# RWKV layer: elementwise work of the channel-major stage from GpSimd to VectorE, and score products that alternate between the halves of TensorE's rows

## The chip, the cores and the metric

The kernel runs on one core of one Trainium2 chip. The metric is the device time of one execution in microseconds (us). Five engines work side by side, each through its own list of instructions in order: TensorE (PE in the profile; PEld is its weight load), VectorE (DVE), ScalarE (ACT), GpSimd (POOL) and SyncE (SP), which here issues the weight transfers. An instruction waits on semaphores until its operands are there and its output buffer is free.

## The reference, cut to what matters

A trunk of two layers over 512 tokens of 1024 channels, in float32. Each layer is a half-step SwiGLU feed-forward, a token mixer, cross-attention into 256 memory tokens, and another half-step feed-forward. The mixer of the first layer is RWKV-7, that of the second a chunked gMLP. The change lies in RWKV-7 alone, which has 16 heads of 64 channels:

```python
dx = token_shift(h) - h
xr, xw, xk = h + dx*mu[0], h + dx*mu[1], h + dx*mu[2]
xv, xa, xg = h + dx*mu[3], h + dx*mu[4], h + dx*mu[5]
x3 = jnp.stack([xr, xk, xv], axis=0)
rkv = jnp.einsum('nbsc,cnd->nbsd', x3, w_rkv.reshape(C, 3, C))
...
k = k * (1.0 + (a - 1.0) * k_a)
def step(state, inp):
    r_t, w_t, k_t, v_t, kk_t, b_t = inp
    sa = jnp.einsum('bhij,bhj->bhi', state, -kk_t)
    state = (state * w_t[:, :, None, :] + sa[..., None] * b_t[:, :, None, :]
             + v_t[..., :, None] * k_t[:, :, None, :])
    y = jnp.einsum('bhij,bhj->bhi', state, r_t)
    return state, y
```

The recurrence over 512 steps is the scan. The result is normalised per head, gated and multiplied by `w_o`.

## The kernel before, in words

A program is nine stages: feed-forward, RWKV, attention, feed-forward, feed-forward, gMLP, attention, feed-forward, final norm. Every large product is made of three: an operand is split into a rounded part `hi`, cast by ScalarE (L93), and the rest `lo = raw - hi`, by VectorE (L98) or, in pieces of 512 columns, by GpSimd (L96); `mm3` then adds hi*hi, hi*lo and lo*hi (L114 to L116). `wload` brings a piece of weight by DMA and splits it. A scheduler puts each engine's instructions into one order from the priorities of the code and its own estimates; it can move them across each other where data allow. A wait at the head of an engine's list holds all that stands behind it.

RWKV works in two parts. In the channel-major stage, channels lie on the partitions and tokens along the rows of a tile. First the token-shift difference `dx` (L908, 16 operations of 128x256) and the three mixes made from it (L911) feed the small decay, rate and gate products (L913 to L916). Then the projections of k, r and v follow, 48 steps of one piece of 512 columns of `w_rkv`: `prepare` loads and splits the weight of a step, and for the first of the two column blocks it makes the mix `xm` (L837), casts it (L862) and subtracts (L863, tile `xs`). The projections' outputs go to `AR` and `BK`, eight tiles of each, 128 channels apiece. Work on finished k blocks is done by generators that are advanced between projection steps: `post_k(nb)` multiplies by rates and decays (L1000 to L1002; the norm of each head goes through TensorE as `pn`, L977; then L1037 to L1039), `post_r(nb)` does r's part (L1052, L1056). For each half `q` of the heads, a triangular inverse of 32x32 blocks is worked out on VectorE by substitution, 30 pairs of L1188 and L1195 whose widths go from 60 and 31 up to 256 and down again, and the blocks are put together on TensorE (L1227). Its result is `TT`.

The scan goes in chunks: 8 per half of the heads, 16 in all, so the loop has 16 steps, `n = 0..15`. A step multiplies the state and values `SV` by the score tile `M` (L1448, first solve product), copies the result to `e1`, multiplies by `TT` (L1464), copies that to `AV` (L1466 VectorE, L1467 ScalarE), updates the state (L1482), and makes the output (L1517, L1518). Meanwhile it prepares the next step: `score(n+1)` multiplies `BK` and `AR` for the two halves of the partitions, `par` 0 and 1, in four products each (L1286), masks them into `M` (L1288, VectorE) and copies two parts (L1289, L1290, ScalarE); `decayed` scales `BK` on GpSimd (L1295); `turned` transposes it (L1301). Between the pieces, `next(fill)` puts in independent products of the memory's keys and values (L114 to L116 with `mT`), and `pump()` advances the gate and normalisation (L1318 to L1321). The scan's first scores are made in `prologue`, while the second inverse still runs. PSUM tiles called `sc` come from a pool of two buffers. `rows[par]` are partitions 0 to 63 and 64 to 127; a product whose operands lie in them uses that half of TensorE's rows.

Of the kernel before, what the change touches and what calls it, by code (L numbers as in the profile page):

```python
# [9 lines left out]
F32 = mybir.dt.float32  # L10
F32R = mybir.dt.float32r
AF = mybir.ActivationFunctionType
ALU = mybir.AluOpType
# [5 lines left out]
T = 512  # L19
# [7 lines left out]
NCH = T // CH  # L27
# [12 lines left out]
class Trunk:  # L40
# [763 lines left out]
    def rwkv_in(self, st, prologue):  # L804

        nc, ins = self.nc, self.ins
        col = lambda i, ct: self.cols[:, i, ct : ct + 1]
        hT = self.hT
        AR, BK = self.AR, self.BK
        self.psp = self.pool(st, "psr", 5, space=PSUM)  # L810
        acc = self.pool(st, "acc", 1, space=PSUM)
        sc = self.sc
# [38 lines left out]
        def prepare(i):  # L851
            if i >= len(steps):
                return
            p, nb, k = steps[i]
            m, wi = projs[p]
            late = p == 2 or (p == 1 and k == 1)
            src = ins["rwkv_w_rkv"][wi, nb, k // 2][:, (k % 2) * 512 : (k % 2) * 512 + 512]
            ws[i] = self.wload(src, 512, nc.gpsimd if late else nc.vector)
            if nb == 0:
                xm = xmix(m, k)  # L860
                xh = xsp.tile([P, 2, T], F32R, tag="xs", name="xs")
                nc.scalar.copy(xh[:, 0], xm)  # L862
                nc.gpsimd.tensor_tensor(xh[:, 1], xm, xh[:, 0].bitcast(F32), ALU.subtract)  # L863
                xs[p, k] = xh[:, 0], xh[:, 1]
# [33 lines left out]
        for half in range(2):  # L898
            s = slice(256 * half, 256 * half + 256)
            for ct in range(KC):  # L900
# [4 lines left out]
                with self.tc.high_priority(offset=60 if early else 0):  # L905
                    dx = room(n)
                    eng = nc.vector if early else nc.gpsimd
                    eng.tensor_tensor(dx, hT[:, ct, s], h, ALU.subtract)  # L908
                    xw, xa, xg = [room(n + j) for j in (1, 2, 3)]
                    for m, z in ((1, xw), (4, xa), (5, xg)):  # L910
                        nc.vector.scalar_tensor_tensor(z, dx, col(MU + m, ct), h, ALU.mult, ALU.add)  # L911
# [77 lines left out]
        def post_k(nb):  # L989
            pn = acc.tile([P, 512], F32, tag="acc", name="pn")  # L990

            def part(i):
# [7 lines left out]
                nc.vector.tensor_tensor(fe, fe, em, ALU.mult)  # L1000
                nc.gpsimd.tensor_tensor(a, a, c3(em), ALU.mult)
                nc.vector.tensor_tensor(c3(fe), raw, c3(fe), ALU.mult)  # L1002
# [23 lines left out]
            for i in range(4):  # L1026
# [10 lines left out]
                nc.vector.scalar_tensor_tensor(c3(kn), raw, nkk[:, ct : ct + 1], c3(ps), ALU.mult, ALU.mult)  # L1037
                nc.gpsimd.tensor_tensor(raw, c3(kn), c3(ep[:, 0:T]), ALU.mult)
                nc.vector.tensor_tensor(a, a, c3(kn), ALU.mult)  # L1039
# [196 lines left out]
    def rwkv_scan(self, st):  # L1236
# [42 lines left out]

        def score(n, M, par):  # L1280

            q, c = divmod(n, NCH)
            ps = sc().rearrange("p (k j) -> p k j", k=4)
            for i in range(4):
                ct = 4 * q + i
                mm(ps[:, i], BK[ct][rows[par], c, :], AR[ct][rows[par], c, :], start=True, stop=True)  # L1286
            mA = self.con[:, I_MA : I_MA + P].unsqueeze(1).to_broadcast([P, 4, P])
            nc.vector.tensor_tensor(M[:, par], ps, mA, ALU.mult)  # L1288
            nc.scalar.copy(M[rows[par], par, :, 0:64], self.ARq[q][rows[par], :, c, 0:64])  # L1289
            nc.scalar.copy(rz[n % 2][rows[par], par], self.ARq[q][rows[par], :, c, 64:128])  # L1290

# [68 lines left out]
        def prologue():  # L1360
# [5 lines left out]
            yield  # L1366
            score(0, M, 0)
            yield
            score(0, M, 1)
            decayed(0)  # L1370
# [53 lines left out]
        for n in range(2 * NCH):  # L1424
# [30 lines left out]
            if not end:  # L1455
                score(n + 1, nm, 0)
            next(fill, None)
            pump()
            for s in range(2):
# [7 lines left out]
                nc.scalar.copy(AV[rows[1], 1, cs, :], p2[rows[1]])  # L1467
            if not end:
                score(n + 1, nm, 1)
                if c + 2 != NCH:  # L1470
                    decayed(n + 1)
            next(fill, None)
# [260 lines left out]
```

## Time and profile before

| what | value |
|---|---|
| median of 3 runs | 2445.85 us (2445.23 to 2446.88) |
| the profiled execution's own time | 2445.8 us |
| its span in the trace | 2444.0 us |
| mean granted TensorE clock, share of full speed | 0.992 |
| busy: PE / DVE / ACT / POOL | 2382.0 / 1690.0 / 1087.3 / 236.6 us |
| chain that ended last: PE / DVE / ACT | 88% / 6% / 2% |
| the RWKV channel-major stage | 365 to 645 us |
| its scan | 645 to 818 us |

The profiled execution agrees with the median; 1.8 us of its time lie outside the span. TensorE is busy for 97% of the span, but that is a mean over stages: the waits are nearly all in the channel-major stage. Busy times of engines overlap, so they don't add up to the span.

### The profile page before, as it was taken

The numbers are of one execution on the slowest core, as the hardware profiler recorded it, in microseconds if no ns is written. First come the engines' busy times: TensorE is split into PE (matmuls) and PEld (weight loads), VectorE is DVE, ScalarE is ACT, GpSimd is POOL, SyncE is SP. The second block draws the span as 40 slices with busy tenths as digits, with TensorE's granted clock in tenths as the row PEclk, the third lists the DMA queues.
The fourth block names the chain that finished last, engine by engine and source line by source line (L and its number), as shares of the span: only waits on it lengthen the run. The fifth ranks groups of instructions, "written<-read, shape, count | busy, mean of one in ns | idle before, by whom it ended". The sixth has DMA issues, their size and how long they took to land.

```text
span 2444.0 us, 40275 instructions
## 1 busy us (share of the span) xinstructions
PE 2382.0 (97%) x16336; PEld 2085.6 (85%) x16336; DVE 1690.0 (69%) x2607; ACT 1087.3 (44%) x1821; POOL 236.6 (10%) x230
## 2 busy tenths in 40 slices
PE   7999999888899999999999999999999999999998
PEld 7898985656787888989898999998888888989897
DVE  7776858788767655969595877674253464969594
ACT  5343434875455344535254534343342343535252
POOL 2000004433345200000000000000000000000000
PEclk9999999999999999999999999999999999999999
DMA  4433232111434432233232324242322232233232
GB/s 148 142 100 121 87 102 72 61 44 57 123 87 120 154 101 74 83 102 120 78 125 94 118 70 130 78 151 86 104 87 88 85 121 82 70 104 112 93 95 86
DMA packets 104938, 241.66 MB, mean 99 GB/s; under 512 B 27184, under 2 KB 31280, under 8 KB 104368
## 3 DMA queue, kind: packets, MB, share of 16 engines
q1 hardware_dynamic: 98864, 225.67, 29.3%
q10 hardware_dynamic: 5888, 13.42, 1.7%
q8 instruction: 128, 2.10, 0.4%
q14 instruction: 58, 0.48, 0.1%
HBM read 227.38 MB, written 7.34 MB: 96 GB/s over the span
## 4 chain that ended last, share of the span: by engine, by line
PE 88%; DVE 6%; ACT 2%; issue 1%; DMA 1%; POOL 1%; DVEq 0%; POOLq 0%; SPq 0%; ACTq 0%
PE ps L114 27%; PE ps L116 27%; PE ps L115 27%; PE sc L1286 1%; DVE tmp L1188 1%; PE ps L217 1%; DVE X L1195 1%; PE y L1517 1%; DVE AR L911 1%; PE y L1518 1%; DVE wlo L98 1%; PE ps L756 1%; POOL wlo L96 0%; PE sm L1448 0%; DMA m_scr<-mo 0%
## 5 line engine op out<-in xcount | busy, mean ns | idle before, releaser
L98 DVE TENSOR_TENSOR wlo<-wraw,whi 128x1024 fp32r<-128x1024 f32 (+1 forms) x246 | 277.4, 1131 | 296.9 <-ACT whi L93 278.3
L114 PE MATMUL ps<-nT_hi,whi 128*128 128x256 f32 (+1 forms) x1504 | 449.6, 301 | 3.5 <-ACT nT_hi L93 1.5
L116 PE MATMUL ps<-nT_hi,wlo 128*128 128x256 f32 (+1 forms) x1504 | 448.4, 299 | 1.2 <-POOL wlo L96 1.2
L115 PE MATMUL ps<-nT_lo,whi 128*128 128x256 f32 (+1 forms) x1504 | 449.0, 299 | 0.4 <-DVE nT_lo L98 0.3
L93 ACT CAST whi<-wraw 128x1024 fp32r<-128x1024 f32 (+1 forms) x268 | 245.9, 921 | 370.6 <-PE ps L116 237.5
L114 PEld LDWEIGHTS ps<-nT_hi,whi 128*128 128x128 f32 x1504 | 283.1, 189 | 15.1 <-ACT nT_hi L93 3.2
L115 PEld LDWEIGHTS ps<-nT_lo,whi 128*128 128x128 f32 x1504 | 284.4, 189 | 10.8 <-DVE nT_lo L98 1.5
L116 PEld LDWEIGHTS ps<-nT_hi,wlo 128*128 128x128 f32 x1504 | 284.0, 189 | 11.3 <-POOL wlo L96 1.5
L116 PE MATMUL ps<-whi,hT_lo 128*128 128x512 f32 x704 | 278.2, 395 | 0.0
L114 PE MATMUL ps<-whi,hT_hi 128*128 128x512 f32 x704 | 278.0, 395 | 0.0
L115 PE MATMUL ps<-wlo,hT_hi 128*128 128x512 f32 x704 | 277.9, 395 | 0.0
L116 PE MATMUL ps<-s_hi,wlo 128*128 128x256 f32 x960 | 271.2, 283 | 1.2 <-DVE wlo L98 1.1
L114 PE MATMUL ps<-s_hi,whi 128*128 128x256 f32 x960 | 271.0, 282 | 1.3 <-ACT whi L93 0.7
L115 PE MATMUL ps<-s_lo,whi 128*128 128x256 f32 x960 | 270.3, 282 | 0.0
L93 ACT CAST whi<-g_raw 128x1024 fp32r<-128x1024 f32 x160 | 168.1, 1050 | 201.7 <-PE ps L116 135.6
L98 DVE TENSOR_TENSOR wlo<-g_raw,whi 128x1024 fp32r<-128x1024 f32 x160 | 195.4, 1221 | 33.2 <-ACT whi L93 32.3
L116 PEld LDWEIGHTS ps<-s_hi,wlo 128*128 128x128 f32 x960 | 181.6, 189 | 2.0 <-DVE wlo L98 2.0
L114 PEld LDWEIGHTS ps<-s_hi,whi 128*128 128x128 f32 x960 | 181.7, 189 | 1.7 <-ACT whi L93 0.9
L115 PEld LDWEIGHTS ps<-s_lo,whi 128*128 128x128 f32 x960 | 181.4, 189 | 0.0
L197 POOL TENSOR_TENSOR rs<-ms,mhalf 128x1 f32<-128x1 f32 x42 | 26.1, 622 | 1391.2 <-DVE ms L191 1391.2
L116 PEld LDWEIGHTS ps<-whi,hT_lo 128*128 128x128 f32 x704 | 132.5, 188 | 30.9
L115 PEld LDWEIGHTS ps<-wlo,hT_hi 128*128 128x128 f32 x704 | 132.6, 188 | 30.7
(360 smaller groups left out, 4870.7 us busy)
## 6 DMA issues: line engine op xcount, KB each, us to landing
wraw<-in_ffn_w_out_dram SPq DMA_DIRECT2D x88, 512.0 KB, 4.1
g_raw<-in_ffn_w_in_dram SPq DMA_DIRECT2D x80, 512.0 KB, 3.7
t_raw<-in_ffn_w_in_dram SPq DMA_DIRECT2D x80, 256.0 KB, 3.0
e_raw<-in_ffn_w_in_dram SPq DMA_DIRECT2D x80, 256.0 KB, 3.4
wraw<-in_rwkv_w_rkv_dram SPq DMA_DIRECT2D x48, 256.0 KB, 2.8
wraw<-in_ffn_w_in_dram SPq DMA_DIRECT2D x16, 512.0 KB, 3.6
wraw<-in_xattn_wq_dram SPq DMA_DIRECT2D x16, 512.0 KB, 3.6
wraw<-in_xattn_wo_dram SPq DMA_DIRECT2D x16, 512.0 KB, 3.5
```

The lines of the kernel that those rows point to most:

```text
L93: r = [self.nc.scalar.copy(hi, src)]
L98: r.append(self.nc.vector.tensor_tensor(lo, src, hi.bitcast(F32), ALU.subtract))
L114: mm(ps, l[0], r[0], start=start, stop=False, **kw)
L115: mm(ps, l[0], r[1], start=False, stop=False, **kw)
L116: mm(ps, l[1], r[0], start=False, stop=stop, **kw)
L197: self.nc.gpsimd.tensor_tensor(rs, ms, self.mhalf[:, 0:1], ALU.pow)
L217: nc.tensor.transpose(ps[:, j * P : (j + 1) * P], xn[:, k * P : (k + 1) * P], self.ident)
L756: nc.tensor.matmul(pv[:, t * P : (t + 1) * P], v[:, t, g * P : (g + 1) * P], ws[:, g, :], start=True, stop=True,)
L911: nc.vector.scalar_tensor_tensor(z, dx, col(MU + m, ct), h, ALU.mult, ALU.add)
L1188: nc.vector.tensor_tensor(tv, M2[:, s + 1 : 32, s : s + 1].to_broadcast([P, n, s + 1]), X[:, s : s + 1, 0 : s + 1].to_broadcast([P, n, s + ...
L1195: nc.vector.tensor_tensor(xs, xs, tv, ALU.add)
L1286: mm(ps[:, i], BK[ct][rows[par], c, :], AR[ct][rows[par], c, :], start=True, stop=True)
```

## The change

Five places in the channel-major stage that used GpSimd for an elementwise operation use VectorE: the `lo` split of the 18 late weights, the 24 `xs` subtractions, 15 of the 16 `dx`, and the products L1001 and L1038 (8 each). In the scan, `score` is called once per step, after the first solve product: it takes two `sc` tiles and issues its eight products with `par` alternating, then does both masks and the copies. `decayed` stays behind the second solve product. Lines behind 863 move by 1 to 3; those behind the loop in `score` too.

```diff
--- before.py
+++ after.py
@@ -853,14 +853,13 @@
                 return
             p, nb, k = steps[i]
             m, wi = projs[p]
-            late = p == 2 or (p == 1 and k == 1)
             src = ins["rwkv_w_rkv"][wi, nb, k // 2][:, (k % 2) * 512 : (k % 2) * 512 + 512]
-            ws[i] = self.wload(src, 512, nc.gpsimd if late else nc.vector)
+            ws[i] = self.wload(src, 512)
             if nb == 0:
                 xm = xmix(m, k)
                 xh = xsp.tile([P, 2, T], F32R, tag="xs", name="xs")
                 nc.scalar.copy(xh[:, 0], xm)
-                nc.gpsimd.tensor_tensor(xh[:, 1], xm, xh[:, 0].bitcast(F32), ALU.subtract)
+                nc.vector.tensor_tensor(xh[:, 1], xm, xh[:, 0].bitcast(F32), ALU.subtract)
                 xs[p, k] = xh[:, 0], xh[:, 1]
 
 
@@ -904,8 +903,7 @@
                 early = half == 0 and ct < 1
                 with self.tc.high_priority(offset=60 if early else 0):
                     dx = room(n)
-                    eng = nc.vector if early else nc.gpsimd
-                    eng.tensor_tensor(dx, hT[:, ct, s], h, ALU.subtract)
+                    nc.vector.tensor_tensor(dx, hT[:, ct, s], h, ALU.subtract)
                     xw, xa, xg = [room(n + j) for j in (1, 2, 3)]
                     for m, z in ((1, xw), (4, xa), (5, xg)):
                         nc.vector.scalar_tensor_tensor(z, dx, col(MU + m, ct), h, ALU.mult, ALU.add)
@@ -998,7 +996,7 @@
                 act(em, L[:, ct, :], AF.Exp, scale=DECAY)
                 act(c3(fe), a, AF.Identity, scale=col(KA, ct), bias=oka[:, ct : ct + 1])
                 nc.vector.tensor_tensor(fe, fe, em, ALU.mult)
-                nc.gpsimd.tensor_tensor(a, a, c3(em), ALU.mult)
+                nc.vector.tensor_tensor(a, a, c3(em), ALU.mult)
                 nc.vector.tensor_tensor(c3(fe), raw, c3(fe), ALU.mult)
                 halved(ct, 0, c3(fe))
                 return sq
@@ -1035,7 +1033,7 @@
                 kn = tmp("fe")[:, :T]
                 raw, a = AR[ct][:, :, 0:64], AR[ct][:, :, 64:128]
                 nc.vector.scalar_tensor_tensor(c3(kn), raw, nkk[:, ct : ct + 1], c3(ps), ALU.mult, ALU.mult)
-                nc.gpsimd.tensor_tensor(raw, c3(kn), c3(ep[:, 0:T]), ALU.mult)
+                nc.vector.tensor_tensor(raw, c3(kn), c3(ep[:, 0:T]), ALU.mult)
                 nc.vector.tensor_tensor(a, a, c3(kn), ALU.mult)
                 halved(ct, 1, a)
                 yield
@@ -1277,17 +1275,19 @@
         def new_m(n):
             return cps[n % 2].tile([P, 2, 4, P], F32, tag="M", name="M")
 
-        def score(n, M, par):
+        def score(n, M):
 
             q, c = divmod(n, NCH)
-            ps = sc().rearrange("p (k j) -> p k j", k=4)
+            pss = [sc().rearrange("p (k j) -> p k j", k=4) for _ in range(2)]
             for i in range(4):
                 ct = 4 * q + i
-                mm(ps[:, i], BK[ct][rows[par], c, :], AR[ct][rows[par], c, :], start=True, stop=True)
+                for par, ps in enumerate(pss):
+                    mm(ps[:, i], BK[ct][rows[par], c, :], AR[ct][rows[par], c, :], start=True, stop=True)
             mA = self.con[:, I_MA : I_MA + P].unsqueeze(1).to_broadcast([P, 4, P])
-            nc.vector.tensor_tensor(M[:, par], ps, mA, ALU.mult)
-            nc.scalar.copy(M[rows[par], par, :, 0:64], self.ARq[q][rows[par], :, c, 0:64])
-            nc.scalar.copy(rz[n % 2][rows[par], par], self.ARq[q][rows[par], :, c, 64:128])
+            for par, ps in enumerate(pss):
+                nc.vector.tensor_tensor(M[:, par], ps, mA, ALU.mult)
+                nc.scalar.copy(M[rows[par], par, :, 0:64], self.ARq[q][rows[par], :, c, 0:64])
+                nc.scalar.copy(rz[n % 2][rows[par], par], self.ARq[q][rows[par], :, c, 64:128])
 
         def decayed(n):
             q, c = divmod(n, NCH)
@@ -1364,9 +1364,8 @@
             cur = load_v(0)
             M = new_m(0)
             yield
-            score(0, M, 0)
-            yield
-            score(0, M, 1)
+            score(0, M)
+            yield
             decayed(0)
             yield
             self.mem_load()
@@ -1453,7 +1452,7 @@
                     nc.vector.tensor_copy(e1, p1)
                 es.append(e1)
             if not end:
-                score(n + 1, nm, 0)
+                score(n + 1, nm)
             next(fill, None)
             pump()
             for s in range(2):
@@ -1465,10 +1464,8 @@
                 cs = slice(2 * s, 2 * s + 2)
                 nc.vector.tensor_copy(AV[rows[0], 0, cs, :], p2[rows[0]])
                 nc.scalar.copy(AV[rows[1], 1, cs, :], p2[rows[1]])
-            if not end:
-                score(n + 1, nm, 1)
-                if c + 2 != NCH:
-                    decayed(n + 1)
+            if not end and c + 2 != NCH:
+                decayed(n + 1)
             next(fill, None)
             pump()
             if not last:
```

Where the instructions stand. The first place is on TensorE, in one scan step of the second half of the heads: `sm` are the PSUM tiles of the small products, `sc` those of the scores, and `ps` with `whi` and `mT` are fill. A tile's size in such a row is the space it is given, not what one product writes. Before:

```order
L1448 MATMUL sm_8104<-SV_7956,M_7962 64x64 x4
L1286 MATMUL sc_8111<-AR1_3886,BK1_3894 128x128 x4
L114 MATMUL ps_7732<-whi_7987,mT_6158 128x512
...
L1464 MATMUL sm_8133<-e1_8102,TT1_6916 64x64 x4
L1464 MATMUL sm_8140<-e1_8109,TT1_6916 64x64 x4
L1286 MATMUL sc_8147<-AR1_3886,BK1_3894 128x128 x4
L114 MATMUL ps_7733<-whi_7987,mT_6158 128x512
L115 MATMUL ps_7733<-wlo_7988,mT_6158 128x512
L116 MATMUL ps_7733<-whi_7987,mT_6158 128x512
L1482 MATMUL sm_8162<-AV_7957,BT_8079 64x64 x4
```

Now:

```order
L1447 MATMUL sm_8104<-SV_7956,M_7962 64x64 x4
L1285 MATMUL sc_8111<-AR1_3886,BK1_3894 128x128
L1285 MATMUL sc_8112<-AR1_3886,BK1_3894 128x128
L1285 MATMUL sc_8111<-AR1_3886,BK1_3894 128x128
L1285 MATMUL sc_8112<-AR1_3886,BK1_3894 128x128
...
L1285 MATMUL sc_8112<-AR1_3886,BK1_3894 128x128
L114 MATMUL ps_7740<-whi_7995,mT_6158 128x512
...
L1463 MATMUL sm_8141<-e1_8102,TT1_6916 64x64 x4
L1463 MATMUL sm_8148<-e1_8109,TT1_6916 64x64 x4
L114 MATMUL ps_7741<-whi_7995,mT_6158 128x512
...
L114 MATMUL ps_7740<-whi_8048,mT_6158 128x512
L1479 MATMUL sm_8162<-AV_7957,BT_8079 64x64 x4
```

The second group of four scores has gone from behind L1464 (now L1463) to the first, where they alternate between two `sc` tiles; between L1463 and L1479 (before L1482) there is fill alone.

The second place is on VectorE where `post_k(0)` begins, with the splits of projection weights around it. Before:

```order
L98 TENSOR_TENSOR wlo<-wraw,whi 128x512
L947 SCALAR_TENSOR_TENSOR L<-fe,sq 128x512
L1000 TENSOR_TENSOR fe<-fe,em 128x512
L98 TENSOR_TENSOR wlo<-wraw,whi 128x512
L1002 TENSOR_TENSOR fe<-AR_3885,fe 128x512
L98 TENSOR_TENSOR wlo<-wraw,whi 128x512
L1000 TENSOR_TENSOR fe<-fe,em 128x512
L1002 TENSOR_TENSOR fe<-AR_3885,fe 128x512
L837 SCALAR_TENSOR_TENSOR xm_4779<-hT,omu,xm_4777 128x512
```

Now:

```order
L98 TENSOR_TENSOR wlo<-wraw,whi 128x512
L945 SCALAR_TENSOR_TENSOR L<-fe,sq 128x512
L998 TENSOR_TENSOR fe<-fe,em 128x512
L999 TENSOR_TENSOR AR_3885<-AR_3885,em 128x8x64
L1000 TENSOR_TENSOR fe<-AR_3885,fe 128x512
L98 TENSOR_TENSOR wlo<-wraw,whi 128x512 x2
L998 TENSOR_TENSOR fe<-fe,em 128x512
L999 TENSOR_TENSOR AR_3885<-AR_3885,em 128x8x64
L1000 TENSOR_TENSOR fe<-AR_3885,fe 128x512
L862 TENSOR_TENSOR xs<-xm_4655,xs 128x512
L862 TENSOR_TENSOR xs<-xm_4704,xs 128x512
L837 SCALAR_TENSOR_TENSOR xm_4779<-hT,omu,xm_4777 128x512
```

L999 (before L1001 on GpSimd) stands between L998 and L1000, which do not need it, and two `xs` subtractions (L862, before L863 on GpSimd) and more `wlo` splits are in line.

The third place is on VectorE in the second inverse (`tmp`, `X`), where the first scores of the scan are masked into `M`. Before:

```order
L1195 TENSOR_TENSOR X<-X,tmp 128x9x23
L1188 TENSOR_TENSOR tmp<-M_5896,X 128x192
L1195 TENSOR_TENSOR X<-X,tmp 128x8x24
L1188 TENSOR_TENSOR tmp<-M_5896,X 128x175
L1195 TENSOR_TENSOR X<-X,tmp 128x7x25
L1188 TENSOR_TENSOR tmp<-M_5896,X 128x156
L98 TENSOR_TENSOR mT<-mraw,mT 128x512
L1288 TENSOR_TENSOR M<-sc,con 128x512 x2
L98 TENSOR_TENSOR mT<-mraw,mT 128x512
L1195 TENSOR_TENSOR X<-X,tmp 128x6x26
```

Now:

```order
L1193 TENSOR_TENSOR X<-X,tmp 128x17x15
L98 TENSOR_TENSOR wlo<-wraw,whi 128x512
L1186 TENSOR_TENSOR tmp<-M_5896,X 128x256
L1193 TENSOR_TENSOR X<-X,tmp 128x16x16
L1186 TENSOR_TENSOR tmp<-M_5896,X 128x255
L1193 TENSOR_TENSOR X<-X,tmp 128x15x17
L1186 TENSOR_TENSOR tmp<-M_5896,X 128x252
L98 TENSOR_TENSOR mT<-mraw,mT 128x512
L98 TENSOR_TENSOR wlo<-wraw,whi 128x512
L1288 TENSOR_TENSOR M<-sc,con 128x512 x2
L98 TENSOR_TENSOR mT<-mraw,mT 128x512
L1193 TENSOR_TENSOR X<-X,tmp 128x14x18
```

The masks L1288 stand behind the step of 252 elements, where they stood behind that of 156; in between there are `wlo` splits that GpSimd did before.

## Rows read from the trace of the kernel before

**Rows 1.** Windows by stage: us, busy time of each engine (instructions), PEclk, DMA share, GB/s.
```profile
365.00:645.00 280.00, 245.08 (x1709) 168.74 (x1708) 225.97 (x348) 168.97 (x293) 113.81 (x103) 0.94 0.21 64
645.00:818.00 173.00, 171.75 (x2145) 143.96 (x2143) 125.05 (x247) 89.58 (x213) 82.00 (x72) 1.00 0.41 104
```

In these rows the engines are in the order PE, PEld, DVE, ACT, POOL.

**Rows 2.** Windows inside the channel-major stage, same columns.
```profile
365.00:470.00 105.00, 102.10 (x479) 67.04 (x478) 80.66 (x116) 65.58 (x112) 45.33 (x44) 1.00 0.21 67
470.00:500.00 30.00, 23.30 (x304) 14.63 (x302) 19.14 (x23) 22.72 (x40) 15.23 (x15) 0.77 0.12 37
500.00:565.00 65.00, 53.65 (x193) 36.29 (x194) 63.90 (x111) 42.42 (x72) 22.17 (x19) 0.95 0.18 57
597.00:645.00 48.00, 41.35 (x188) 32.40 (x179) 40.66 (x75) 15.89 (x30) 16.31 (x15) 0.93 0.33 98
```

**Rows 3.** Groups of POOL, 365 to 645: busy us, mean ns | idle before, releaser.
```profile
L863 POOL TENSOR_TENSOR xs<-xm,xs 128x512 fp32r<-128x512 f32 x24 | 37.0, 1546 | 43.5 <-ACT xs L862 43.4
L96 POOL TENSOR_TENSOR wlo<-wraw,whi 128x512 fp32r<-128x512 f32 x18 | 24.5, 1364 | 55.2 <-ACT whi L93 52.4 <-issue 2.8
L1001 POOL TENSOR_TENSOR AR<-AR,em 128x512 f32<-128x512 f32 x8 | 14.8, 1850 | 28.0 <-ACT fe L999 22.5 <-DVE wlo L98 5.5
L1038 POOL TENSOR_TENSOR AR<-fe,em 128x512 f32<-128x512 f32 x8 | 12.0, 1502 | 3.5 <-DVE fe L1037 3.1
```

**Rows 4.** Groups of DVE, 365 to 645, same columns.
```profile
L1188 DVE TENSOR_TENSOR tmp<-M,X 128x60 f32<-128x60 f32 (+15 forms) x60 | 29.3, 489 | 1.3
L98 DVE TENSOR_TENSOR wlo<-wraw,whi 128x512 fp32r<-128x512 f32 x32 | 26.8, 841 | 8.3 <-ACT whi L93 4.3 <-POOL rz L1383 4.0
L1195 DVE TENSOR_TENSOR X<-X,tmp 128x60 f32<-128x60 f32 (+15 forms) x60 | 25.6, 426 | 1.2
L837 DVE SCALAR_TENSOR_TENSOR xm<-hT,omu,xm 128x512 f32<-128x512 f32 x24 | 23.6, 1000 | 2.5 <-POOL xs L863 2.4
L911 DVE SCALAR_TENSOR_TENSOR AR<-AR,cols,hT 128x256 f32<-128x256 f32 x45 | 22.2, 561 | 0.1
```

**Rows 5.** Single lines, 365 to 645: duration ns min/median/max, first and last start.
```profile
L1000 DVE TENSOR_TENSOR fe<-fe,em x8: 676/932/1820, 450.0 to 515.8; 128x512 f32<-128x512 f32 x8
L837 DVE SCALAR_TENSOR_TENSOR xm<-hT,omu,xm x24: 735/748/1781, 406.7 to 592.7; 128x512 f32<-128x512 f32 x24
L911 DVE SCALAR_TENSOR_TENSOR AR<-AR,cols,hT x45: 469/477/1397, 381.0 to 411.6; 128x256 f32<-128x256 f32 x45
```

**Rows 6.** Timeline of DVE in the second inverse: start, duration.
```profile
617.56 0.42 DVE L1195 TENSOR_TENSOR X<-X,tmp 128x256 f32<-128x256 f32 x1
```

**Rows 7.** The chain that ended last, 450 to 542: start, us, what.
```profile
450.00 1.80 POOL AR L1001
...
462.09 1.73 POOL xs L863
...
498.68 1.83 DVE fe L1000
...
541.12 1.49 DVE X L1195
```

**Rows 8.** Waits of PE, 365 to 645: us, times, longest.
```profile
PE sc L1301 <- DVE M L1288: 6.7, 1, 6.7
```

**Rows 9.** Timeline of PE in one scan step: start, us from the first to the last end.
```profile
769.58 0.68 PE L1464 MATMUL sm<-e,TT 64*64 64x64 f32 x16
770.19 1.16 PE L1286 MATMUL sc<-AR,BK 64*128 64x128 f32 x8
771.27 0.50 PE L114 MATMUL ps<-whi,mT 128*128 128x512 f32 x1
...
772.17 0.69 PE L1482 MATMUL sm<-AV,BT 128*64 128x64 f32 x16
```

**Rows 10.** Timelines of DVE and ACT in the same step.
```profile
771.38 0.69 DVE L1288 TENSOR_TENSOR M<-sc,con 128x512 f32<-128x512 f32 x1
...
770.60 0.46 ACT L1467 COPY AV<-sm 64x128 f32<-64x128 f32 x2 [1.55 <-DVE AV L1466]
```

## Prediction

> **What bounds the kernel now.** I read the busy time by stage first. The feed-forward, attention and gMLP parts ahead of 365 us and behind 818 us hold none of the edited lines, so I leave them as they are. In the 173 us of the scan TensorE is busy 171.75: it has no slack, and only less work on TensorE shortens it. In the 280 us of the channel-major stage ahead TensorE is busy 245.08, so 35 us are waits; VectorE (DVE) is busy 225.97, GpSimd (POOL) 113.81 [rows 1].
>
> Next I cut that stage where its character changes. From 365 to 470 TensorE is busy 102.10 of 105: the other engines hide behind the projections. From 470 to 500 it is idle 6.7 of 30, and its mean granted clock is 0.77. From 500 to 565 VectorE is busy 63.90 of 65, so VectorE sets the pace. From 597 to 645 TensorE is idle 6.65 of 48 [rows 2]. These three stretches are where the moved operations can matter.
>
> The groups of GpSimd's work say what is moved, and what it waited for: the `xs` and `wlo` subtractions wait mostly for ScalarE's casts, 43.4 and 52.4 us in total, L1001 22.5 for ScalarE too [rows 3]. GpSimd has time for that.
>
> **What the moved operations cost VectorE.** By the diff 24 + 18 + 8 + 8 = 58 operations of 128x512 and 15 of 128x256 change engine. VectorE does a 128x512 product or difference undisturbed in 676 ns (the shortest L1000 [rows 5]) to 0.69 us (L1288 [rows 10]), and 128x256 in 0.42 [rows 6]. So 58 x 0.69 + 15 x 0.42 = 40.0 + 6.3 = 46.3 us are added.
>
> **What it gets back.** The same L1000 that takes 676 ns at best takes 1820 at worst, and L837 and L911 have as wide a spread in one shape [rows 5]; the long ones coincide with a GpSimd operation with two inputs. Mean less minimum, times the count: L98 32 x (841 - 676) = 5.3; L837 24 x (1000 - 735) = 6.4; L911 45 x (561 - 469) = 4.1 [rows 4, 5]; L1000 by its median 8 x (932 - 676) = 2.0 [rows 5]. The 120 inverse operations (L1188, L1195) have sizes from 31 to 256 elements, 181 in the mean; at 0.42 us for 256 I estimate 0.35 undisturbed, so 60 x (0.489 - 0.35) + 60 x (0.426 - 0.35) = 12.9 come back, and at least 4.5 if 0.42 held for all [rows 4, 6]. These five come to 30.7 (22.3 at least). So VectorE is loaded by at most 46.3 - 22.3 = 24 us more over the stage, and I take some 10, since groups that I don't list (L1039, L1056) are stretched too. Against that 88 us of slow GpSimd work (37.0 + 24.5 + 14.8 + 12.0 [rows 3]) no longer stands between producer and reader: one takes 1.36 to 1.85 us there and 0.69 on VectorE.
>
> The Trainium skill, SBUF — State Buffer, "Who interferes with whom", says that a VectorE instruction with two SBUF inputs and a GpSimd one that reads SBUF exclude each other for the whole instruction. The trace agrees on which operations are stretched. By the rule alone up to 88 us of VectorE time could come back, twice what is added; the rows give about a third of that, because GpSimd often runs while VectorE waits, and I go by the rows.
>
> **Where that falls.** Four terms:
> - 365 to 470: the 15 differences add 6.3 us to a chain of L911, which gets back 4.1. TensorE has 2.9 us of idle time in all [rows 2], most of it there. I take 1 us lost (0 to 2).
> - 470 to 500: what arrives late here was made between 450 and 470, where the chain runs through GpSimd: L1001 at 450.00 for 1.80 us and `xs` at 462.09 for 1.73, the first and last of four such links [rows 7]. Each is 1.0 shorter on VectorE, so 4 us, of 6.7 that TensorE idles. I take 4 (0 to 7). The second excerpt of the order, on VectorE, shows the other side: L999 and L862 stand in line there, where nothing stood.
> - 500 to 565: VectorE is the pace. The chain has six stretched operations in it, L1000 with 1.83 the first and an inverse step with 1.49 the last, each about 1.0 over its undisturbed time [rows 7]: 6 come back on the chain, and the four L1038 here and their kin are 0.7 shorter each. Against it 14 moved operations of 0.69 (9.7). Between -4 and +7 I take 2.
> - 597 to 645: TensorE's longest wait of the stage is here, 6.7 us, L1301 for the masked scores of L1288 [rows 8], which stand in VectorE's queue behind the second inverse. The third excerpt of the order shows them after the step of 252 elements instead of after that of 156: 16 inverse operations of about 0.40 fewer ahead, 6.4 us. In the whole order six `wlo` splits (three in the excerpt) are new ahead of them inside this inverse, 4.1 us, and about half of the inverses' 12.9 is returned. 6.4 - 4.1 + 6 is more than the wait itself holds; since ahead of the inverse three more splits and five `xs` were put in, partly in idle time, I take 4 (-3 to 6.7).
>
> Sum for the stage: -1 + 4 + 2 + 4 = 9 us gained, bounds -9 and +21.
>
> **The score products.** In each of the 15 loop steps that have a successor, TensorE so far does one group of four products after the first solve product and another after the second, 1.08 us each (770.19 to 771.27, [rows 9]). In a group the products use one half of the rows and follow one another. After the change, eight products stand together, the halves taking turns, into two PSUM tiles. The trace has no such pair of 64 rows by 128 columns, only the nearest thing: the 64x64 products of L1464, which alternate between halves. Their 16 records take 0.61 us (769.58 to 770.19), 0.038 each; L1286's eight take 1.08, 0.135 each, 3.5 times as long for twice the columns. So an alternating pair should cost about as much as one product now, and eight products 1.08 instead of 2.16: 15 x 1.08 = 16.2 us. If halves do not overlap, only a change-over to another kind of product goes, for which I allow 0.2 per step (an estimate: L1464's whole 0.61 leaves no room for much more), 3 us. I take the first, because L1464 shows halves at work at the same time.
>
> What this takes away is cover. TensorE's L1482 needs `AV`, copied from the second solve product. Before, the other score group and a fill (1.08 + 0.90) stood between; now the fill alone, 771.27 to 772.17 [rows 9]. VectorE's two mask products (2 x 0.69), then two ScalarE copies, come ahead of the last `AV` copy (2 x 0.23, [rows 10]). From the scores' end: 1.38 + two copies at 0.4 (an estimate from the 0.46 of [rows 10]) + 0.46 = 2.65; TensorE reaches L1482 after fill, solve and fill, 0.90 + 0.61 + 0.90 = 2.4, later in steps with gate products. So 0.25 per step, 4 us over 15. The scan gains 16 - 4 = 12 (0 to 16).
>
> The Trainium skill, TensorEngine Tiling (Array Packing), "PSUM Bottleneck", says that tiling speeds TensorE but not the evacuation, which may become the bound. By that rule the scan would be paced by the four copies, worked out from rows as the second rival below.
>
> **The sum.** 9 + 12 = 21: 2445.8 (the profiled execution's own time, 1.8 of it outside the span and untouched; the median is 2445.85, so it is a typical one) - 21 = 2424.8 us.
>
> **The rivals.**
> - *The halves do not overlap* (0.14): each score record takes its 0.13 us whichever half. The stage gains 9, the scan 3: 2434. For it: no 64x128 pair is in the trace. Against it: L1464.
> - *The copies pace the scan* (0.15): `AV` is late by 1 us in each step rather than 0.25, because the mask products and the copies in front of it run one after the other over two engines. Then 15 of the 16 are given back: 2445.8 - 9 - 1 = 2436. Against it: TensorE waited for `AV` only once in the scan so far, as VectorE is busy 125.05 of 173 [rows 1].
> - *The other side: VectorE inherits GpSimd's waits* (0.19). GpSimd could sit 43.4 us in 24 and 52.4 us in 18 operations, 2 to 3 us each, for ScalarE's cast [rows 3]; VectorE's queue is in order, so a split whose cast is late holds the inverses behind it. It matters where VectorE sets the pace, 500 to 565 and 597 to 645, with some 24 moved operations. Eight such waits at 3 us are 24: 2424.8 + 24 = 2449; from seven of them on the gain is gone. Against it: the 32 splits that VectorE has already waited for ScalarE only 4.3 us in all [rows 4], and ScalarE is busy only 15.89 of 48 at the end [rows 2].
>
> **Chances.** Forecast 0.52, then 0.14, 0.15, 0.19. A measurement of this kernel tells about 0.2% (4.9 us) from no change: the first three are faster (0.81); of the last I give 0.09 to no change, 0.10 to slower. The range for 8 in 10 runs from 2408 (the stage at +19, the scan at 16 would be 2411, a little beyond) to 2443, which takes in both smaller gains and leaves out most of the last rival. The likeliest case alone has 2410 to 2432.
>
> **What would show it.** L98, L837, L1188 and L1195 at nearly their undisturbed times, and POOL with hardly any work in the stage; L1301's wait for `M` under 3 us; the stage some 271 us long. In the scan one run of 16 score records in about 1.1 us, periods of TensorE's steps some 0.8 shorter, and a small wait of L1482 for `AV`. It would be wrong if the 16 records take 2 us, if L1482 waits a microsecond in most steps, or if VectorE idles before L98 or `xs` for ScalarE while inverse steps are in line.

## The result, and the profile after

The changed kernel takes 2410.47 us (median of 4, 2409.73 to 2414.22), beside 2445.54 for the kernel before on the same chip: a ratio of 0.9858, 95% interval 0.9843 to 0.9873, so 35 us less. The forecast was 21 less. The time lies in its range, but the 35 us are not made up as forecast: the stage gave 31.8 us where 9 were forecast, the scan 5.3 where 12 were.

In the page of the kernel after, the first line has each engine's busy time, share of the span and instructions:

```profile
PE 2359.3 (98%) x16336; PEld 2067.2 (86%) x16336; DVE 1677.4 (70%) x2680; ACT 1087.9 (45%) x1821; POOL 136.4 (6%) x157
```

VectorE has 73 operations more and is busy 12.6 us less than before (1690.0). TensorE does the same 16336 matmuls in 22.7 us less.

The windows by stage, of before and of after, cut where the layer's input is copied and where the first scan step and the output product begin (columns as in [rows 1]). Before:

```profile
365.80:646.58 280.78, 245.86 (x1712) 169.12 (x1710) 225.51 (x348) 170.03 (x294) 113.81 (x103) 0.94 0.21 65
646.58:817.40 170.82, 169.57 (x2133) 142.56 (x2133) 124.44 (x245) 87.90 (x210) 82.00 (x72) 1.00 0.41 102
```

After, and two stretches inside the first stage, against the same hours in [rows 2]:

```profile
366.70:615.72 249.02, 233.00 (x1712) 161.14 (x1710) 213.43 (x419) 168.47 (x294) 14.97 (x30) 0.97 0.23 73
615.72:781.20 165.48, 159.28 (x2135) 131.83 (x2133) 123.49 (x248) 88.15 (x211) 79.36 (x72) 0.99 0.43 106
...
470.00:500.00 30.00, 29.08 (x350) 19.90 (x349) 25.21 (x44) 29.07 (x52) 0.45 (x4) 1.00 0.16 49
500.00:565.00 65.00, 55.34 (x304) 37.93 (x304) 61.91 (x127) 43.27 (x71) 3.07 (x10) 0.92 0.20 64
```

The stage ahead of the scan is 31.8 us shorter, the scan 5.3. In the stage TensorE's idle time falls from 34.9 to 16.0 us (of 62.0 and 48.7 in the whole span, so before somewhat more than half of the waits lay here, not nearly all), and its busy time from 245.86 to 233.00 with the same 1712 matmuls: most of the second is the clock, whose mean rises from 0.94 to 0.97. From 470 to 500 TensorE idled 6.7 us at 0.77 before; now it idles 0.9 at 1.00.

The groups of VectorE in the stage answer to [rows 4]; L1186 and L1193 are the inverse, L909 the mixes:

```profile
L98 DVE TENSOR_TENSOR wlo<-wraw,whi 128x512 fp32r<-128x512 f32 x49 | 33.5, 685 | 6.0 <-ACT whi L93 5.7
L1193 DVE TENSOR_TENSOR X<-X,tmp 128x60 f32<-128x60 f32 (+15 forms) x60 | 20.6, 343 | 0.9
L1186 DVE TENSOR_TENSOR tmp<-M,X 128x60 f32<-128x60 f32 (+15 forms) x60 | 20.5, 342 | 1.0
L909 DVE SCALAR_TENSOR_TENSOR AR<-AR,cols,hT 128x256 f32<-128x256 f32 x45 | 18.9, 477 | 0.1
L837 DVE SCALAR_TENSOR_TENSOR xm<-hT,omu,xm 128x512 f32<-128x512 f32 x24 | 17.6, 747 | 0.1
L862 DVE TENSOR_TENSOR xs<-xm,xs 128x512 fp32r<-128x512 f32 x24 | 16.2, 685 | 0.9 <-ACT xs L861 0.9
```

Every mean shown has come down to the undisturbed time: the inverse from 489 and 426 ns to 342 and 343, L837 from 1000 to 747, L98 from 841 to 685. The new `xs` subtractions wait for ScalarE 0.9 us in all, where GpSimd waited 43.4.

When each inverse starts and ends is read from the block transposes around it, by line (ns min/median/max, then first and last start). Before, and after:

```profile
L1178 DVE STREAM_TRANSPOSE M<-MD x2: 2051/2077/2103, 502.2 to 597.7; 128x1024 f32<-128x1024 f32 x2
L1205 DVE STREAM_TRANSPOSE A<-X x2: 2094/2183/2272, 570.0 to 634.8; 128x1024 f32<-128x1024 f32 x2
```

```profile
L1176 DVE STREAM_TRANSPOSE M<-MD x2: 2029/2033/2037, 493.2 to 579.3; 128x1024 f32<-128x1024 f32 x2
L1203 DVE STREAM_TRANSPOSE A<-X x2: 2107/2114/2120, 554.1 to 615.0; 128x1024 f32<-128x1024 f32 x2
```

So 9.0 us are gained up to the first inverse, 6.9 in it (67.8 to 60.9), 2.5 between the two, 1.4 in the second, and 11.1 from there to the first scan step (11.8 to 0.7); that is 30.9, and 31.8 with the 0.9 by which the stage began later.

One scan step of TensorE, the same as in [rows 9], and the waits of TensorE in the scan:

```profile
732.32 0.69 PE L1447 MATMUL sm<-SV,M 128*64 128x64 f32 x16
732.93 1.16 PE L1285 MATMUL sc<-AR,BK 64*128 64x128 f32 x16
734.03 0.50 PE L114 MATMUL ps<-whi,mT 128*128 128x512 f32 x1
...
737.75 0.45 PE L1479 MATMUL sm<-AV,BT 128*64 128x64 f32 x8
738.13 0.50 PE L115 MATMUL ps<-wlo,mT 128*128 128x512 f32 x1
738.47 0.40 PE L116 MATMUL ps<-whi,mT 128*128 128x512 f32 x1
738.79 0.45 PE L1479 MATMUL sm<-AV,BT 128*64 128x64 f32 x8
```

```profile
PE sm L1479 <- ACT AV L1466: 1.9, 4, 1.2
PE sm L1463 <- DVE e L1452: 1.7, 1, 1.7
PE sc L1301 <- POOL BK L1295: 1.6, 1, 1.6
```

Sixteen score records take 1.10 us (732.93 to 734.03), as eight did. But there are new waits (before, TensorE waited once in the scan, 1.2 us for `AV`), and the state update L1479 comes in two pieces with fill between.

### The profile page after: what moved, and what is told of

It is laid out like the page before. It is cut to its first block, busy times and chain, and to the rows that moved or that the text cites. A ratio compares the mean times of both kernels' runs of the same rounds, so it can differ in the third digit from the quotient of the medians.

```text
span 2408.0 us, 40219 instructions
## 1 busy us (share of the span) xinstructions
PE 2359.3 (98%) x16336; PEld 2067.2 (86%) x16336; DVE 1677.4 (70%) x2680; ACT 1087.9 (45%) x1821; POOL 136.4 (6%) x157
## 4 chain that ended last, share of the span: by engine, by line
PE 89%; DVE 5%; ACT 3%; DMA 1%; issue 1%; POOL 1%; DVEq 0%; SPq 0%; POOLq 0%; ACTq 0%
PE ps L114 27%; PE ps L116 27%; PE ps L115 27%; PE ps L217 1%; DVE wlo L98 1%; PE y L1514 1%; PE y L1515 1%; PE ps L756 1%; PE sc L1285 0%; ACT whi L93 0%; POOL wlo L96 0%; DMA m_scr<-mo 0%; PE ps L911 0%; PE sm L1479 0%; ACT BK L983 0%
## 5 line engine op out<-in xcount | busy, mean ns | idle before, releaser
L98 DVE TENSOR_TENSOR wlo<-wraw,whi 128x1024 fp32r<-128x1024 f32 (+1 forms) x264 | 281.3, 1069 | 292.5 <-ACT whi L93 277.9
L98 DVE TENSOR_TENSOR wlo<-g_raw,whi 128x1024 fp32r<-128x1024 f32 x160 | 196.5, 1228 | 32.6 <-ACT whi L93 31.9
L114 PEld LDWEIGHTS ps<-whi,hT_hi 128*128 128x128 f32 x704 | 132.6, 188 | 30.3
```

What stands on the lines that cost most here:

```text
L98: r.append(self.nc.vector.tensor_tensor(lo, src, hi.bitcast(F32), ALU.subtract))
L114: mm(ps, l[0], r[0], start=start, stop=False, **kw)
```

## The experiments

Twelve kernels ran, in three groups; the kernel before, run beside each, had medians of 2445.1, 2445.1 and 2446.0. Line numbers differ by up to 15 among them.

**The two halves of the change, each by itself.** Theory A: the stage and the scan gain separately what the traces show. Theory B: part of the stage's gain comes with the score change, which moves the first masks. The first kernel has the changed lines of the stage, with `score` and its calls as before; the second has only the new `score` and its calls, some of which are:

```diff
-            score(0, M, 0)
-            yield
-            score(0, M, 1)
+            score(0, M)
...
-                score(n + 1, nm, 0)
+                score(n + 1, nm)
```

> Only the operations moved from GpSimd to VectorE; the score products as before. Theory A (the stage gains by itself what the two traces show, 31 us before the scan, and the scan 5): about 2414 us, the first scan step at about 616. Theory B (the early start of the scan comes in part from the new place of the first masks, which the score change brings with it): 2420 to 2430. The forecast's own terms would give 2436.

> Only the score products changed; the elementwise operations on GpSimd as before. Theory A: 2436 to 2441, all of it in the scan. Theory B: 2425 to 2432, with the stage ahead shorter too. By the forecast's term for the scan 2434.

Measured: 2418.59 (ratio 0.9894, 0.9877 to 0.9910) and 2436.37 (0.9964, 0.9951 to 0.9977): 26.6 and 8.8 us less, 35.4 in sum. The first and last start of the first solve product show where, moves alone and scores alone:

```profile
L1446 PE MATMUL sm<-SV,M x256: 222/222/271, 612.7 to 777.1; 128*64 128x64 f32 x128
```

```profile
L1449 PE MATMUL sm<-SV,M x256: 222/222/271, 644.0 to 797.2; 128*64 128x64 f32 x128
```

The stage begins at 364.4 and 364.5 in these two (before at 365.8), so with the moves alone it is 248.3 long, 32.5 less than before, but the scan is 164.4 long instead of 161.3. The score change alone shortens the scan to 153.2 and the stage by 1.3. The first median lies between the ranges of the two theories; the lengths of the stage decide for A: it loses 32.5 by the moves alone and 31.8 in the changed kernel, and B has at most the 1.3.

**The moves in two groups.** One kernel moves only the 42 splits, one only the 16 products of `post_k`:

```diff
-            ws[i] = self.wload(src, 512, nc.gpsimd if late else nc.vector)
+            ws[i] = self.wload(src, 512)
...
-                nc.gpsimd.tensor_tensor(xh[:, 1], xm, xh[:, 0].bitcast(F32), ALU.subtract)
+                nc.vector.tensor_tensor(xh[:, 1], xm, xh[:, 0].bitcast(F32), ALU.subtract)
```

```diff
-                nc.gpsimd.tensor_tensor(a, a, c3(em), ALU.mult)
+                nc.vector.tensor_tensor(a, a, c3(em), ALU.mult)
...
-                nc.gpsimd.tensor_tensor(raw, c3(kn), c3(ep[:, 0:T]), ALU.mult)
+                nc.vector.tensor_tensor(raw, c3(kn), c3(ep[:, 0:T]), ALU.mult)
```

> Only the 42 subtractions of the splits (18 wlo, 24 xs) moved to VectorE. If the gain of the stage comes from contention, which goes with the number of GpSimd operations, 42 of 73 and the longest in total (61.5 of 99.5 us) bring some 18 of the 31 us: 2427. If the gain lies in the chain through the products of post_k, under 8: above 2437.

> Only the 16 products of post_k (L1001, L1038) moved to VectorE. By contention alone 26.8 of 99.5 us of GpSimd time, some 8 of 31 us: 2437. If the chain through these products is the cause, 15 or more: 2430 or less.

Measured: 2429.00 (0.9936, 0.9921 to 0.9951) and 2438.66 (0.9975, 0.9964 to 0.9986), 16.1 and 6.5 us less. All moves together gave 26.6; the 15 `dx` did not run by themselves, so the 4.0 that are left are theirs or come from the groups together. The gain goes with the GpSimd time removed (0.26, 0.24 and 0.27 us for each us), as contention would have it; but a longer way through GpSimd would grow with that time too, so this alone doesn't part the two. The products, though they stand in the chain [rows 7], are not worth more than their share.

**Contention without the wait for GpSimd.** The changed kernel, with an idle twin on GpSimd of each moved operation:

```diff
+        scr = ep_.tile([P, 256], F32, name="scr")
+        def twin(y, x=None):
+            x = self.con[:, 0:512] if x is None else x
+            for j in range(0, y.shape[-1], 256):
+                nc.gpsimd.tensor_tensor(scr, x[:, j : j + 256], y[:, j : j + 256], ALU.subtract)
```

and, as its counterpart, twins that write and read one column:

```diff
+                nc.gpsimd.tensor_copy(scr[:, 0:1], y[:, j : j + 1])
+                for _ in range(2):
+                    nc.gpsimd.memset(scr, 0.0)
```

> The changed kernel, and in addition GpSimd does an idle twin of each of the 73 operations, in pieces of 128x256 with two inputs from SBUF, started by the same cast or product, into a scratch tile that nobody reads. It brings back the contention without the wait for GpSimd's result. If contention is what the stage gained from: 2425 to 2433. If it was the longer way through GpSimd: under 2416.

> The same, but each piece is a one-column copy and two fills of 128x256, which read nothing. If two operations that read are what gets in each other's way, 2409 to 2413; if any work of GpSimd beside VectorE costs, as e7.

Measured: 2462.66 (1.0075, 1.0059 to 1.0091) and 2416.74 (0.9885, 0.9868 to 0.9903). The reading twins cost 52 us against the changed kernel, and end above the kernel before; the writing ones 6. The first lies 30 us above its range, the second 4 above the range for reads as the cause: the direction is that of contention, the size was not foreseen. Windows of the stage, with the reading twins:

```profile
366.70:667.26 300.56, 253.07 (x1701) 171.35 (x1699) 263.08 (x418) 166.31 (x289) 138.96 (x161) 0.90 0.19 59
```

and with the writing ones:

```profile
366.70:623.96 257.26, 234.65 (x1714) 161.48 (x1712) 216.69 (x420) 168.38 (x293) 152.00 (x423) 0.97 0.22 71
```

GpSimd is busy about as long in both, and VectorE has the same work: 263 us against 217 (after: 213). Nobody reads the twins' results, but the tiles that they read stay taken until then: ScalarE and SyncE wait for that some 14 us in the first kernel and 15 in the second, so it is not what sets them apart. VectorE's own time, stretched by GpSimd's reads, made the scan start 51.5 us later.

**What the added work costs.** The changed kernel without the 42 subtractions: where they stood, `hi` is used for `lo`.

```diff
-                nc.vector.tensor_tensor(xh[:, 1], xm, xh[:, 0].bitcast(F32), ALU.subtract)
-                xs[p, k] = xh[:, 0], xh[:, 1]
+                xs[p, k] = xh[:, 0], xh[:, 0]
...
-            ws[i] = self.wload(src, 512)
+                    nc.scalar.copy(hi, raw)
+                ws[i] = hi, hi
```

> The changed kernel unaltered, for comparison with the others on this chip: 2408 to 2414.

> The changed kernel without the 42 subtractions that it moved (18 wlo, 24 xs): the rounded part stands in for the rest in these products, so the output is not the reference's; TensorE does the same work. It takes 42 x 0.685 = 28.8 us from VectorE. If VectorE sets the pace nearly throughout the stage, 20 to 29 us less: 2382 to 2391. If the added operations lie in idle time or beside TensorE's own work, under 12 less: above 2398.

Measured: 2410.35 for the changed kernel again (2408.28 to 2415.45), and 2406.57 without the splits (0.9840, 0.9827 to 0.9854). The stage without them:

```profile
366.70:614.00 247.30, 232.43 (x1707) 162.68 (x1706) 194.80 (x379) 167.58 (x292) 14.81 (x30) 0.98 0.23 74
```

VectorE is busy 18.6 us less and TensorE idles as long as in the changed kernel (14.9, after 16.0). The second inverse's last L1203 starts at 602.6 instead of 615.0, but the scan starts no sooner: from 602 to its start TensorE is busy without a gap. In this state TensorE and its clock, with short chains between engines, are what is left. The 4 us are near what these runs can tell.

**The alternation, and the place of the scores.** All four products of one half and then of the other; and the alternating eight behind the second solve product:

```diff
-            for i in range(4):
-                ct = 4 * q + i
-                for par, ps in enumerate(pss):
+            for par, ps in enumerate(pss):
+                for i in range(4):
+                    ct = 4 * q + i
```

```diff
-            if not end:
-                score(n + 1, nm)
             next(fill, None)
             pump()
...
-            if not end and c + 2 != NCH:
-                decayed(n + 1)
+            if not end:
+                score(n + 1, nm)
+                if c + 2 != NCH:
+                    decayed(n + 1)
```

> The changed kernel, its eight score products in the same place but first all four of one half, then all four of the other. Theory A (halves at work side by side are what the scan gains): 15 x 1.08 less the change-over are lost again, 2421 to 2426. Rival (the gain comes from one place instead of two, and the first mask can now start a microsecond earlier): 2411 to 2416.

> The changed kernel with the eight alternating products behind the second solve product, ahead of decayed, where they stand between it and the state update that waits for AV. If the waits of TensorE in the scan (5 us in the trace, L1479 for AV and L1463 for e1 among them) come from masks and copies queued ahead of AV, 2 to 5 us are gained: 2405 to 2408. If the masks are then late for the next step or for the transpose, 2411 to 2418.

Measured: 2414.43 (0.9870, 0.9852 to 0.9887; the four runs lie between 2409 and 2419) and 2416.74 (0.9886, 0.9870 to 0.9902). Without alternation, on TensorE:

```profile
697.10 1.71 PE L1285 MATMUL sc<-AR,BK 64*128 64x128 f32 x16
698.74 0.39 PE L114 MATMUL ps<-mT,whi 128*128 128x256 f32 x1
```

Sixteen records take 1.64 us, not 2.16 and not 1.10: the second half's first products start while the first half's last are at work. So order decides over half a microsecond per step, 8 us over 15. In the trace, which is of the longest of the four runs, the scan is 7.2 us longer than in the changed kernel (163.1 and 155.9 from the first to the last start of the first solve product). The median loses 4: that is in the rival's range, but since half of the overlap comes without alternation, not for the rival's reason; the wide runs leave the size of the loss in the median open. The late scores, one step, and a wait:

```profile
740.60 1.16 PE L1285 MATMUL sc<-AR,BK 64*128 64x128 f32 x8
741.68 0.51 PE L114 MATMUL ps<-whi,mT 128*128 128x512 f32 x1
...
742.58 1.16 PE L1285 MATMUL sc<-AR,BK 64*128 64x128 f32 x8
```

```profile
PE sc L1285 <- DVE v L1325: 1.3, 1, 1.3
```

In steps with gate products (L1318 to L1321, in an `sc` tile until L1325) the eight fell apart into two groups with fill between, and the overlap was gone; the scan is 6.6 us longer than in the changed kernel. Two `sc` tiles at once are all that the pool has: that place needs the tile the gate holds. The time lies in the second range, but not for its reason: the run says nothing on the masks.

**Two trials to go lower.** The first `e1` copy on ScalarE, and `decayed` on VectorE:

```diff
-                if s:
+                if s or n == 0:
                     nc.scalar.copy(e1, p1)
```

```diff
-            nc.gpsimd.tensor_tensor(b, b, D[:, cof(q), c : c + 1].to_broadcast([P, 4, P]), ALU.mult)
+            nc.vector.tensor_tensor(b, b, D[:, cof(q), c : c + 1].to_broadcast([P, 4, P]), ALU.mult)
```

> The changed kernel, where the first scan step's first e1 copy is done by ScalarE, not by VectorE behind the two block transposes of the second inverse (L1203, L1206). If that copy's wait of 1.7 us and the lower clock after it make the first step 3 us longer than the score change alone has it (12.05 against 8.85), 2 to 4 us less than the changed kernel. If the mask products behind the same transposes are next in line, within 1 us of it.

> The changed kernel with the scan's decayed product (L1295) on VectorE too. If GpSimd's reading slows VectorE's queue here as well and the transpose's wait for BK (1.6 us) goes, 1 to 4 us less than the changed kernel. If VectorE's queue, ahead of AV and the masks, is what the scan waits for, 1 to 5 us more.

Measured: 2410.42 (0.9853, 0.9839 to 0.9866) and 2410.18 (0.9855, 0.9842 to 0.9869), neither apart from the changed kernel. A wait of TensorE in the first of them:

```profile
PE y L1515 <- DVE AV L1465: 1.8, 1, 1.8
```

The wait for `e1` is gone, and the next copy behind the same transposes is late by as much. In the second the wait for `BK` (1.6 us) is gone and a wait for a `wlo` split of 1.8 has come.

## Why the forecast was right, and where its sizes were wrong

**The sign and the mechanism** held: the moved operations came cheaply, because VectorE got back at least as much as it took on. That the time lies in the range is in part luck: the stage's 31.8 us are beyond its own bound of 21, and a scan that gave 7 less than forecast made up for some of it; with the forecast's 12 from the scan the time would have been about 2404, below the range.

**What it gets back**, 30.7 us, was right for the five groups listed. Working the sum again with the means of after: L98 32 x (841 - 685) = 5.0, L837 24 x (1000 - 747) = 6.1, L911 45 x (561 - 477) = 3.8, the inverse 60 x (489 - 342) + 60 x (426 - 343) = 13.8, and L1000 8 x (1098 - 690) = 3.3 (its means, where the prediction took the median): 32. Too small was what the groups not listed add: 14 (L1039 3.2, L1056 2.7, L947 1.6 and others), not the 6 or so that the "some 10" implied. So 46 us came back in the lengths of the same operations, and 45 were added by the 71 new ones that lie in the stage. That VectorE's busy time there fell by 12.1 all the same is for 8 of it another thing: an operation right behind another overlaps it in the record, in the changed kernel for example

```profile
462.21 0.69 DVE L1000 TENSOR_TENSOR fe<-AR,fe 128x512 f32<-128x512 f32 x1
462.81 0.69 DVE L98 TENSOR_TENSOR wlo<-wraw,whi 128x512 fp32r<-128x512 f32 x1
```

so it takes 0.60 us of busy time rather than 0.69, and there are 295 such pairs instead of 203. For operations that stand so, the prediction's cost of 0.69 each was a little high. The Trainium skill, SBUF — State Buffer, "Who interferes with whom", has the conflict between a two-input VectorE operation and a GpSimd one that reads, and none with one that only writes. The two kernels with twins agree, 263 against 217 us. What came back, 46, is about half of the bound of 88, where the prediction took a third from rows.

**Where that falls** failed most: 9 us were taken, 31.8 came. Up to 500 the terms were -1 and +4; the first inverse started 9 earlier. The row of 470 to 500 had shown it: the wait there came with a granted clock of 0.77, and I priced the wait alone. TensorE's busy time for the same matmuls fell by 12.9 us in the stage, which is in none of the four terms. Some 10 of it are the clock. It was granted at 0.50 in five stretches of the stage before and in two after; their sums, and TensorE's busy time in them:

```profile
sum 34.14, PE 29.41; mean PE 5.88
sum 13.65, PE 8.62; mean PE 4.31
```

So 20.8 us less were worked at half clock, which costs about half of that (an estimate from the products at both clocks in the last section). Another 1.0 is the scan's first scores, which now alternate. The last term, 4, was mis-sized in part for the same reason: from the second inverse to the scan 11.1 were gained, of which the wait of L1301 for the masks (6.7, after 0.4) is 6.3. The 500 to 565 term, 2, answers to 6.9 in the first inverse. But here the change has its price as well. TensorE's longest wait of the changed stage is for VectorE's L1054 (6.9 us, before 1.9), with the moved L1036 in the queue ahead of it, and the granted clock is 0.50 from 528.4 to 538.6:

```profile
PE pb L975 <- DVE sq L1054: 7.9, 2, 6.9
```

**The score products**: halves work side by side as forecast, 1.10 us for sixteen records. The kernel before had shown part of this where its first scores of both halves follow one another, sixteen records in less than twice 1.08:

```profile
617.71 1.71 PE L1286 MATMUL sc<-AR,BK 64*128 64x128 f32 x16
```

The prediction overlooked that row when it said that the trace has no such pair. Counted from each start to the next product's, without waits, the score records of the scan take 31.5 us before and 17.8 after: 13.7 less, where 16 were forecast. In eleven of the 15 steps they take the 1.10; in the others they are cut or take longer, most of all here, where they come in four pieces (the last at 714.24) and L1285 waits for ScalarE's copy out of an `sc` tile (L1303):

```profile
709.29 0.48 PE L1285 MATMUL sc<-AR,BK 64*128 64x128 f32 x2
710.21 0.71 PE L1285 MATMUL sc<-AR,BK 64*128 64x128 f32 x6 [0.43 <-ACT BT L1303]
...
711.22 0.49 PE L1285 MATMUL sc<-AR,BK 64*128 64x128 f32 x4
```

**What this takes away is cover** was the other mis-sized term: 4 us were to be given back. TensorE idles 5.0 more in the scan (1.2 before, 6.2 after) and its other products take 3.3 more, so of 13.7 the scan kept 5.3, or 8.1 in the kernel with the score change alone (161.3 to 153.2). The waits for `AV` came to 1.9 (forecast 4), but `BK` from GpSimd and `e1` added 3.3. The wait for `e1` belongs to the moves, not to the scores: the start of the scan now meets the end of the second inverse, VectorE's transposes hold `e1`, and the lower clock follows. The kernel with the moves alone has it too, 1.6 us, and its scan is 3.1 longer than before. Of the 3.3 the lower clock, 3.4 us of it in the scan, explains up to half; the rest is open. That L1479 is cut in two, as in the step shown, is not it: TensorE goes from one line's products to another's as often as before, 640 times. The Trainium skill, TensorEngine Tiling (Array Packing), "PSUM Bottleneck", warns that evacuation may become the next bound; the trace has it in part, 1.9 us of `AV` waits.

**The rivals.** Halves overlap, so the first is out. The copies delayed TensorE four times in the scan, not in each step. The other side, VectorE inheriting GpSimd's waits, did not come: `xs` waited 0.9 us and L98 5.7 for ScalarE in 73 operations.

**What stays open**: how the stage's 31.8 us divide between contention and the longer way through GpSimd. No kernel kept GpSimd's results without its reads. Contention alone can be of this size: reading twins cost 46 us more than writing ones, with some 124 us of GpSimd work where the moved operations had 99.5; but VectorE carries more in those kernels than in the one before. The direct waits of VectorE for GpSimd's results in [rows 4] are small (2.4 for `xs`; the 4.0 are for a memset of `rz`, which was not moved). So contention is likely the larger part; more is not shown.

## What to carry to other kernels

Before giving an elementwise operation with two inputs to an idle GpSimd, take mean less minimum of VectorE's operations in the same stretch: what they lose can be as much as they were spared (here 46 us against 45). Where TensorE waits and its granted clock is down in the same window, price the matmuls behind the wait at both clocks, not the wait alone. Products that use half of TensorE's rows belong side by side in turn, but look at what they covered, and whether their buffers are free at the new place.

## What the runs showed of the hardware that was not expected

The same time of VectorE was worth nothing and everything: 18.6 us less of it in the stage, without the splits, started the scan at 615.3, where the two profiles of the changed kernel have 615.7 and 614.3; 49.7 us more, with the reading twins, started it 51.5 later.

A short wait of TensorE cost more than itself. In the first scan step of the changed kernel, on TensorE:

```profile
617.56 0.28 PE L115 MATMUL ps<-mT,whi 128*128 128x256 f32 x1
617.68 0.28 PE L116 MATMUL ps<-mT,wlo 128*128 128x256 f32 x1
619.64 0.45 PE L1463 MATMUL sm<-e,TT 64*64 64x64 f32 x8 [1.68 <-DVE e L1452]
...
621.41 0.41 PE L114 MATMUL ps<-mT,whi 128*128 128x256 f32 x1
621.62 0.41 PE L115 MATMUL ps<-mT,whi 128*128 128x256 f32 x1
```

After the wait of 1.68 us the same product of 256 columns shows 0.41 us instead of 0.28 and starts every 0.21 instead of every 0.12: the lower of the two clock levels, 1.2 instead of 2.4 GHz. It lasts until about 624, where the granted clock is 1.00 again. The step took 12.05 us (11.00 in the second profile of this kernel); it took 8.85 in the kernel with the score change alone and in the one without splits.

Products of different halves start side by side even when not alternated, but only at the seam: 1.64 us for sixteen records, 1.10 in turn.
